# A two-layer trunk: the down projection's Strassen products in groups of three row pairs, an up product after each

## The chip, the cores and the metric

The kernel runs on one core of a Trainium2 chip. The metric is the device time of one execution in microseconds (us). A profile of one further execution gives every instruction of the engines: PE (TensorE, matmuls) with PEld (its weight loads), DVE (VectorE), ACT (ScalarE), POOL (GpSimd) and SP (SyncE, which issues the DMAs).

## The reference, cut to what matters

512 tokens of width 1024 pass through two layers, each a mixer (pooling, then stick-breaking attention) and a squared-ReLU MLP with 4096 hidden rows, all in float32. The MLP is what the change is about:

```python
def sq_relu_mlp(h, w_up, w_down):
    u = jnp.matmul(h, w_up)
    return jnp.matmul(jnp.square(jax.nn.relu(u)), w_down)
...
        h = rms_norm(x, mlp_pre_g[layer])
        x = x + rms_norm(sq_relu_mlp(h, w_up[layer], w_down[layer]), mlp_post_g[layer])
```

## The kernel before

**Precision.** A float32 matrix product is made of three matmuls in the fp32r format: each operand is split into a high part (ACT copies it with rounding, L188, or L118 for a weight) and a low part (DVE subtracts the high part, L189, or L120), and high x high, high x low and low x high are added in PSUM. `mm3` (L209 to L211) and `up_block` (L534 to L536) write these three. One product of 128x128 by 128x512 is called a matmul of 128x512 below.

**Weights.** `want` lists the weights in the order of use. `make` takes the next: SP loads it into one of two raw tiles (L108), ACT and DVE (POOL for four of them) split it. `fill` does so while fewer than four are made ahead; `get` hands one out. The weights of the attention layer get their gains on POOL first (L130).

**The MLP.** The hidden rows stand in 32 blocks of 128. An up product makes one block for all 512 tokens: 24 matmuls, then relu (L489) and square (L490) on ACT. The down product of blocks 0 to 27 is done with Strassen's scheme in Winograd's form, blocks 28 to 31 plainly in `contract`. In the scheme two blocks (2q and 2q+1) make a pair: the two blocks by the two halves of the tokens are the four left quadrants, the two blocks by the two halves of the 1024 output columns the four right ones. Seven products stand for eight. Their left operands (r11, s3, s2, r22, s1, r12, s4) are quadrants or sums of quadrants of the squares, made on POOL (L403 to L406, names s and r in the profile); their right operands (w11, t3, t2, t4, t1, w21, w22) are quadrants or differences of the down weights, made on DVE (L423, names t, xn, spare). All are split into high and low parts.

**Groups.** Before, a group is two pairs (four blocks). `Seven.__init__` loads its four weight blocks, 512 KB each (L384), into the three norm tiles `xn` and a spare tile; `feed` makes the left operands of a pair as its squares come; `prepare` makes the right operands one at a time in eight buffers `w`, called by `make` at most two at a time. `add_to` writes the seven products in one piece: 12 matmuls each (2 token tiles, 2 pairs, 3 matmuls; L456) and two evacuations of a PSUM bank into y (L473 on DVE; for the first sum of a part L471 on ACT). Products that share a PSUM bank keep adding up in it.

**Order.** The program's order is a priority. The library plans the order of each engine's instructions with a simulation of estimated times, so instructions of one group and the next may come interleaved.

**Around it.** `Update` does the sandwich norm: it writes into a norm tile from `xn_tile`, and `transpose` turns it for the next stage (L281). In the attention layer `mix_pair` splits the output of a pair of heads into `ohl` tiles; three of the eight lie in the norm tiles. The out projection then adds them up with `contract`.

Of the kernel before, what the change touches and what calls it, by code (L numbers as in the profile page):

```python
# [10 lines left out]
F32 = mybir.dt.float32  # L11
F32R = mybir.dt.float32r
# [10 lines left out]
GRP = 4  # L23
HEADS = 16
# [37 lines left out]
def trunk(ctx, tc, x, consts, gcol, grow, pw, wup, wdn, wq, wk, wv, wo, out):  # L62
# [26 lines left out]

    def xn_tile():  # L90
        return work.tile([P, D], F32, tag="xn", bufs=3, name=name("xn"))
# [65 lines left out]
    def fill(n=1):  # L157
        if gate[0]:
            behind.update(latest)
        for _ in range(n):  # L160
            if queue and len(made) < ahead and (queue[0][0][0] != "dn" or dn_pool[0] is not None):
                make()
# [130 lines left out]
    def contract(lhs, w, y, first, update=None, tiles=range(T), soon=False):  # L293
# [4 lines left out]
        for t in tiles:  # L298
# [26 lines left out]
            else:  # L325
                product(0, range(last + 1))
            evacuate(0)
# [5 lines left out]
            elif normed and t == T - 1:  # L333
                if not soon:
                    ups[0].transpose()
# [26 lines left out]
    class Seven:  # L362
# [11 lines left out]

        PRODUCTS = (
# [4 lines left out]
        def __init__(self, l, g, mp):  # L380
            self.mp, self.rows, self.left, self.right = mp, [], {}, {}
            self.raw = [xn_tile(), xn_tile(), xn_tile(), spare_tile()]
            for j, raw in enumerate(self.raw):
                nc.sync.dma_start(raw, wdn[l, g * GRP + j])  # L384
            self.rest = self.prepare()

        def feed(self, r):

            q, second = divmod(len(self.rows), 2)
            self.rows.append(r)  # L390
            tile = lambda n, tag: self.mp.tile([P, 2, n], F32R, tag=tag, bufs=2, name=name(tag))
            lo, hi = slice(0, S // 2), slice(S // 2, S)
            if not second:
                a = self.left["r11", q] = tile(S // 2, "r11")
                split(r[:, lo], a[:, 0], a[:, 1])
                return
            a = tile(S, "r2")
            split(r, a[:, 0], a[:, 1])
            self.left["r12", q], self.left["r22", q] = a[:, :, lo], a[:, :, hi]
            r1 = self.rows[-2]  # L400
            sums = self.mp.tile([P, 2, S], F32, tag="s", name=name("s"))
            s2, s3, s1, s4 = sums[:, 0, lo], sums[:, 0, hi], sums[:, 1, lo], sums[:, 1, hi]
            nc.gpsimd.tensor_tensor(out=s3, in0=r1[:, lo], in1=r1[:, hi], op=ALU.subtract)  # L403
            nc.gpsimd.tensor_tensor(out=s1, in0=r1[:, hi], in1=r[:, hi], op=ALU.add)  # L404
            nc.gpsimd.tensor_tensor(out=s2, in0=s1, in1=r1[:, lo], op=ALU.subtract)  # L405
            nc.gpsimd.tensor_tensor(out=s4, in0=r[:, lo], in1=s2, op=ALU.subtract)  # L406
            for n, (x, y) in enumerate((("s2", "s3"), ("s1", "s4"))):
                a = tile(S, f"s{n}")
                split(sums[:, n], a[:, 0], a[:, 1])
                self.left[x, q], self.left[y, q] = a[:, :, lo], a[:, :, hi]  # L410

        def prepare(self):


            def part(key, q, src):
                w = self.right[key, q] = self.mp.tile([P, D], F32R, tag="w", bufs=8, name=name("w"))
                split(src, w[:, NS[0]], w[:, NS[1]])

            def temp():
                return self.mp.tile([P, 512], F32, tag="t", bufs=3, name=name("t"))  # L420

            def combine(out, x, y, op):
                nc.vector.tensor_tensor(out=out, in0=x, in1=y, op=op)  # L423
                return out
# [466 lines left out]
```

## Time and profile before

| | |
|---|---|
| median of 3 runs | 994.76 us (992.62 to 996.26) |
| the profiled execution | 996.64 us, span 994.8 us from the first to the last instruction |
| mean granted TensorE clock | 0.984 |
| moved by DMA | 94.50 MB |

The span has five stretches: the pooling mixer to about 44 us, the first MLP to about 375, attention to about 650, the second MLP to about 970, and the last norm and store. A line of the profile names the source line, the engine, the operation, output and inputs by the program's names, shapes, and count; then busy time, the mean of one in ns, and the idle time just before with what ended it.

### The profile page before, as it was taken

The page shows a single profiled execution, that of the slowest core. Times are in us where ns is not written, and L with a number is a line of the kernel's source. Part 1 is how long each engine was busy: PE and PEld are TensorE (multiplying, and loading weights), DVE is VectorE, ACT ScalarE, POOL GpSimd, SP SyncE. Part 2 cuts the span into 40 slices and gives each one's busy share as a digit, 9 for nine tenths or more (in the row PEclk, how much of TensorE's full clock was granted, in tenths as well). Part 3 has the DMA queues.
Part 4 walks back from the last instruction along what each step waited for, and adds up shares of the span by engine and source line. Part 5 has one row for each costly group of instructions (what it writes and reads, how often), then busy time and mean ns, then how long its engine had stood idle before and what let it go on. Part 6 is the DMA issues. An engine that isn't in the chain of part 4 may idle for free.

```text
span 994.8 us, 12988 instructions
## 1 busy us (share of the span) xinstructions
PE 954.4 (96%) x4823; PEld 810.8 (82%) x4823; DVE 780.6 (78%) x1067; ACT 557.0 (56%) x1005; POOL 252.2 (25%) x238
## 2 busy tenths in 40 slices
PE   7898999999999999999999999989999999999997
PEld 5896888888888888888788988788888888888886
DVE  5987788878877747488688889989778878888636
ACT  5656546456455446566667576658556455464532
POOL 1642202112021147241252300436212021121103
PEclk8998999999999999999999999999999999999999
DMA  7254323323232230112222221144323233231202
GB/s 267 85 162 135 106 86 107 109 103 106 85 111 81 85 127 22 62 45 64 64 73 69 64 72 65 65 148 149 110 102 111 84 125 105 85 127 64 64 22 85
DMA packets 26991, 94.50 MB, mean 95 GB/s; under 512 B 3120, under 2 KB 3504, under 8 KB 26928
## 3 DMA queue, kind: packets, MB, share of 16 engines
q1 hardware_dynamic: 26928, 93.68, 28.2%
q8 instruction: 38, 0.62, 0.2%
q14 instruction: 25, 0.20, 0.1%
HBM read 91.57 MB, written 2.10 MB: 94 GB/s over the span
## 4 chain that ended last, share of the span: by engine, by line
PE 76%; DVE 8%; ACT 4%; POOL 3%; issue 2%; DMA 1%; POOLq 0%; DVEq 0%; ACTq 0%
PE ps L456 26%; PE ps L535 13%; PE ps L536 13%; PE ps L534 13%; PE ps L209 3%; PE ps L210 2%; PE ps L211 2%; DVE e L752 2%; PE ps L780 1%; DVE l L120 1%; PE ps L770 1%; POOL y L234 1%; DMA xn<-in_wdn 1%; ACT h L118 1%; DVE x L240 1%
## 5 line engine op out<-in xcount | busy, mean ns | idle before, releaser
L535 PE MATMUL ps<-xnl,h 128*128 128x512 f32 (+1 forms) x712 | 262.0, 369 | 4.1 <-DVE xnl L189 4.1
L536 PE MATMUL ps<-xnh,l 128*128 128x512 f32 (+1 forms) x712 | 262.1, 369 | 0.5 <-DVE l L120 0.5
L534 PE MATMUL ps<-xnh,h 128*128 128x512 f32 (+1 forms) x712 | 261.0, 369 | 0.0
L120 DVE TENSOR_TENSOR l<-raw,h 128x1024 fp32r<-128x1024 f32 x101 | 128.8, 1276 | 48.5 <-ACT h L118 48.3
L456 PE MATMUL ps<-w,s 128*128 128x512 f32 x672 | 163.4, 394 | 2.1 <-ACT s L188 1.5
L535 PEld LDWEIGHTS ps<-xnl,h 128*128 128x128 f32 x712 | 134.8, 189 | 26.1 <-DVE xnl L189 4.3
L536 PEld LDWEIGHTS ps<-xnh,l 128*128 128x128 f32 x712 | 134.8, 189 | 22.8 <-DVE l L120 0.7
L456 PEld LDWEIGHTS ps<-w,s 128*128 128x128 f32 x672 | 127.2, 190 | 31.1 <-ACT s L188 2.7
L534 PEld LDWEIGHTS ps<-xnh,h 128*128 128x128 f32 x712 | 134.2, 190 | 21.9
L473 DVE TENSOR_TENSOR y<-ps,y 128x512 f32<-128x512 f32 x180 | 120.1, 688 | 40.5 <-PE ps L456 39.3
L118 ACT CAST h<-raw 128x1024 fp32r<-128x1024 f32 x105 | 110.4, 1053 | 63.9 <-PE ps L535 32.4
L456 PE MATMUL ps<-w,r 128*128 128x512 f32 x504 | 124.3, 390 | 2.4 <-DVE r L189 2.4
L188 ACT CAST w<-t 128x512 fp32r<-128x512 f32 x112 | 69.2, 622 | 80.8 <-PE ps L456 61.0
L456 PEld LDWEIGHTS ps<-w,r 128*128 128x128 f32 x504 | 94.7, 188 | 22.4 <-DVE r L189 2.8
L404 POOL TENSOR_TENSOR s<-r,r 128x256 f32<-128x256 f32 x28 | 28.2, 1008 | 323.9 <-ACT r L490 323.9
L130 POOL TENSOR_TENSOR raw<-raw,gc 128x512 f32<-128x512 f32 x48 | 69.9, 1477 | 145.7 <-DMA raw<-in_wv 68.9
L188 ACT CAST w<-xn 128x512 fp32r<-128x512 f32 x56 | 34.9, 624 | 90.1 <-PE ps L456 80.0
L189 DVE TENSOR_TENSOR w<-t,w 128x512 fp32r<-128x512 f32 x112 | 76.5, 705 | 0.7 <-ACT w L188 0.7
L188 ACT CAST s<-s 128x512 fp32r<-128x512 f32 x56 | 34.6, 620 | 45.6 <-POOL s L405 37.6
L189 DVE TENSOR_TENSOR s<-s,s 128x512 fp32r<-128x512 f32 x56 | 42.5, 763 | 22.0 <-ACT s L188 17.5
L189 DVE TENSOR_TENSOR r<-r,r 128x512 fp32r<-128x512 f32 (+1 forms) x60 | 47.2, 789 | 11.7 <-ACT r L188 11.6
L752 DVE TENSOR_TENSOR_SCAN e<-u,begin 128x1280 f32<-128x1280 f32 x16 | 47.5, 2968 | 8.7 <-ACT u L746 8.5
(138 smaller groups left out, 1577.9 us busy)
## 6 DMA issues: line engine op xcount, KB each, us to landing
raw<-in_wup SPq DMA_DIRECT2D x64, 512.0 KB, 3.5
xn<-in_wdn SPq DMA_DIRECT2D x42, 512.0 KB, 3.6
spare<-in_wdn SPq DMA_DIRECT2D x14, 512.0 KB, 4.1
raw<-in_wdn SPq DMA_DIRECT2D x8, 512.0 KB, 3.5
raw<-in_wv SPq DMA_DIRECT2D x8, 512.0 KB, 3.4
raw<-in_wk SPq DMA_DIRECT2D x8, 512.0 KB, 3.5
raw<-in_wq SPq DMA_DIRECT2D x8, 512.0 KB, 3.5
raw<-in_wo SPq DMA_DIRECT2D x8, 512.0 KB, 3.5
```

Source lines behind the costliest of these rows:

```text
L118: nc.scalar.copy(hi, raw)
L120: on.tensor_tensor(out=lo, in0=raw, in1=hi.bitcast(F32), op=ALU.subtract)
L130: nc.gpsimd.tensor_tensor(out=v[:, h], in0=v[:, h], in1=g[:, h].broadcast_to((P, n // 2, D // n)), op=ALU.mult)
L188: latest["act"] = nc.scalar.copy(hi, src)
L189: latest["dve"] = nc.vector.tensor_tensor(out=lo, in0=src, in1=hi.bitcast(F32), op=ALU.subtract)
L209: nc.tensor.matmul(dst, ah, bh, start=start, stop=False)
L456: nc.tensor.matmul(bank, r[:, a], w_[:, NS[b]], start=start and q == 0 and k == 0, stop=q == 1 and k == 2, skip_group_check=True,)
L473: nc.vector.tensor_tensor(out=part, in0=bank, in1=part, op=ALU.add)
L534: nc.tensor.matmul(pu[:, cols], wh[:, k, :], xnh[:, k, cols], start=k == 0, stop=False)
L535: nc.tensor.matmul(pu[:, cols], wh[:, k, :], xnl[:, k, cols], start=False, stop=False)
L536: nc.tensor.matmul(pu[:, cols], wl[:, k, :], xnh[:, k, cols], start=False, stop=k == KC - 1)
L752: nc.vector.tensor_tensor_scan(out=e[:, ::-1], data0=u[:, 1:][:, ::-1], data1=begin[:, ::-1], initial=0.0, op0=ALU.mult, op1=ALU.max,)
```

## The change

The 14 pairs are taken in five groups of 2, 3, 3, 3 and 3 pairs. `load` brings the first blocks of all pairs of a group with one DMA into a tile w1, the second blocks with another into the three norm tiles, which are now one tile xn3. `left` and `right` make the operands of one product for all pairs at once: the sums overwrite the squares and the weights or one tile e, and go into one of two buffers `a` (left) and `w` (right). `mlp` writes one product, one up product of the next group, and then the operands of the product after the next one; the operands of the next group's first two products come at the end of a group. `product` has 18 matmuls with three pairs, 12 with two. The four plain down weights go into pieces of w1, e and w. The squares of a group lie in one tile r. The transpose of the first tile at the end of the first MLP is written ahead of an evacuation, and the `ohl` tiles get five buffers of their own and a part of e.

```diff
+GROUPS = (2, 3, 3, 3, 3)
+MOST = max(GROUPS)
...
+    xn3 = work.tile([P, 3, D], F32, tag="xn3", name="xn3")
+    turn = [0]
+
     def xn_tile():
-        return work.tile([P, D], F32, tag="xn", bufs=3, name=name("xn"))
+        turn[0] += 1
+        return xn3[:, turn[0] % 3]
...
-            return [dn_pool[0].tile([P, D], F32R, tag="w", bufs=8, name=name(x)) for x in "hl"]
+            return dn_pool[0].pop(0)
...
+            if normed and t == T - 1 and not soon:
+                ups[0].transpose()
             evacuate(0)
...
-                if not soon:
-                    ups[0].transpose()
                 product(1, [0])
...
+        def load(self, second):
+            n = self.n
+            if second:
+                w = self.w2 = xn3
+            else:
+                w = self.w1 = self.mp.tile([P, MOST, D], F32, tag="w1", name=name("w1"))
+            src = wdn[self.l, self.first : self.first + 2 * n].rearrange("(n k) p d -> k p n d", k=2)
+            nc.sync.dma_start(w[:, :n], src[1 if second else 0])
+        def squares(self):
+            self.r = self.mp.tile([P, 2, MOST, S], F32, tag="r", bufs=2, name=name("r"))
+        def part(self, b):
+            return self.r[:, b % 2, b // 2]
+        def left(self, i):
+            n, key = self.n, self.PRODUCTS[i][1]
             lo, hi = slice(0, S // 2), slice(S // 2, S)
+            r11, r21, r12, r22 = (self.r[:, k, :n, h] for k in range(2) for h in (lo, hi))
+            if i == 0:
+                self.s1 = self.mp.tile([P, MOST, S // 2], F32, tag="s1", name=name("s1"))
+            s1 = self.s1[:, :n]
+            sub = lambda out, x, y, op=ALU.subtract: nc.gpsimd.tensor_tensor(out=out, in0=x, in1=y, op=op)
+            if key == "s3":
+                sub(s1, r21, r22, ALU.add)
+                sub(r21, r11, r21)
+                sub(r11, s1, r11)
+            elif key == "r22":
+                sub(r11, r12, r11)
+            src = {"r11": r11, "s3": r21, "s2": r11, "r22": r22, "s1": s1, "r12": r12, "s4": r11}[key]
+            a = self.mp.tile([P, 2, MOST, S // 2], F32R, tag="a", bufs=2, name=name("a"))
+            split(src, a[:, 0, :n], a[:, 1, :n])
+            return a
+        def right(self, i):
+            n, key = self.n, self.PRODUCTS[i][2]
+            w11, w12, w21, w22 = (w[:, :n, h] for w in (self.w1, self.w2) for h in NS)
+            if i == 0:
+                self.e = self.mp.tile([P, MOST, 512], F32, tag="e", name=name("e"))
+            e = self.e[:, :n]
+            combine = lambda out, x, y, op=ALU.subtract: nc.vector.tensor_tensor(out=out, in0=x, in1=y, op=op)
+            if key == "t3":
+                combine(e, w22, w12)
+            elif key == "t2":
+                combine(e, e, w11, ALU.add)
+            elif key == "t4":
+                combine(e, w21, e)
+            elif key == "t1":
+                combine(w12, w12, w11)
+            src = {"w11": w11, "t3": e, "t2": e, "t4": e, "t1": w12, "w21": w21, "w22": w22}[key]
+            w = self.mp.tile([P, 2, MOST, 512], F32R, tag="w", bufs=2, name=name("w"))
+            split(src, w[:, 0, :n], w[:, 1, :n])
+            return w
+        def make(self, i):
+            self.operands[i] = self.left(i), self.right(i)
+        def product(self, i, y, first):
+            a, w = self.operands.pop(i)
+            at, _, _, tokens, half = self.PRODUCTS[i]
+            start = at not in self.banks
+            if start:
+                self.banks[at] = [ps(), ps()]
+            for t, bank in enumerate(self.banks[at]):
+                for q in range(self.n):
+                    for k, (x, z) in enumerate(((0, 0), (0, 1), (1, 0))):
                         nc.tensor.matmul(
+                            bank, a[:, x, q, TS[t]], w[:, z, q], start=start and q == 0 and k == 0,
+                            stop=q == self.n - 1 and k == 2, skip_group_check=True,
                         )
+                part = y[2 * tokens + t][:, NS[half]]
+                if first and (tokens, half, t) not in first:
+                    nc.scalar.copy(part, bank)
+                    first.add((tokens, half, t))
+                else:
+                    nc.vector.tensor_tensor(out=part, in0=bank, in1=part, op=ALU.add)
...
+        groups = [Seven(l, firsts[g], n, mp) for g, n in enumerate(GROUPS)]
...
+        groups[0].load(0)
+        groups[0].squares()
         need(0, 1)
-        first = [(ps(), get(("up", l, j))) for j in range(GRP)]
+        n0 = 2 * GROUPS[0]
+        first = [(ps(), get(("up", l, j))) for j in range(n0)]
         for j, (pu, w) in enumerate(first):
-            if j == GRP - 1:
+            if j == n0 - 1:
                 need(2, 3)
+                groups[0].load(1)
             up_block(pu, w, slice(0, S // 2))
         for j, (pu, w) in enumerate(first):
             up_block(pu, w, slice(S // 2, S))
             up(j, pu)
-            feed(j)
-        for g in range(last):
-            up((g + 1) * GRP)
-            del squares[:GRP]
-            group.make(1)
-            group.add_to(y, g == 0)
-            group = Seven(l, g + 1, mp) if g + 1 < last else None
-            feed(0)
-            for j in range(1, GRP):
-                up((g + 1) * GRP + j)
-                feed(j)
-        w = [get(("dn", l, last * GRP + j)) for j in range(GRP)]
+        for i in range(2):
+            groups[0].make(i)
+        for g, group in enumerate(groups):
+            coming = groups[g + 1] if g + 1 < len(groups) else None
+            if coming:
+                coming.squares()
+            ups = list(range(firsts[g + 1], firsts[g + 1] + 2 * GROUPS[g + 1]) if coming else range(plain, NJ))
+            for i in range(7):
+                group.product(i, y, written if g == 0 else None)
+                if i + 2 < 7:
+                    if ups:
+                        up(ups.pop(0))
+                    group.make(i + 2)
+                    if i + 2 == 4 and coming:
+                        coming.load(0)
+                    if i + 2 == 6 and coming:
+                        coming.load(1)
+                else:
+                    if ups:
+                        up(ups.pop(0))
+                    if coming:
+                        coming.make(i + 2 - 7)
+                    elif i == 5:
+                        piece = lambda tag, k, bufs=1: mp.tile([P, k, D], F32R, tag=tag, bufs=bufs, name=name("dn"))
+                        w, e, x, z = piece("w1", 3), piece("e", 1), piece("w", 3, 2), piece("w", 3, 2)
+                        dn_pool[0] = [
+                            [w[:, 0], w[:, 1]], [w[:, 2], e[:, 0]], [x[:, 0], x[:, 1]], [x[:, 2], z[:, 0]],
+                        ]
+        w = [get(("dn", l, j)) for j in range(plain, NJ)]
+        dn_pool[0] = None
         fill(ahead)
-        contract(squares, w, y, False, update)
-        dn_pool[0] = None
+        contract(squares[1:], w, y, False, update)
...
-            if p in (2, 3, 4):
-                both = work.tile([P, D], F32R, tag="xn", bufs=3, name=name("ohl"))
+            if p < PAIRS - 1:
+                both = ap.tile([P, D], F32R, tag="ohl", bufs=5, name=name("ohl"))
             else:
-                both = ap.tile([P, D], F32R, tag="ohl", bufs=3, name=name("ohl"))
+                both = ap.tile([P, NSEG], F32R, tag="e", name=name("ohl"))[:, :D]
...
-    nc = bacc.Bacc("TRN2", target_bir_lowering=False, num_devices=1, dynamic_dma_scratch_size=1024)
+    nc = bacc.Bacc("TRN2", target_bir_lowering=False, num_devices=1, dynamic_dma_scratch_size=256)
```

More of the change, by code (lines that the diff above doesn't have):

```diff
@@ L160, in fill @@
         for _ in range(n):
[L161 removed]
+            if queue and len(made) < ahead and (queue[0][0][0] != "dn" or dn_pool[0]):
                 make()
@@ L480, in mlp @@
         y = y_tiles()
-        last = NJ // GRP - 1
-        squares, group = [], Seven(l, 0, mp)
+        firsts = [2 * sum(GROUPS[:g]) for g in range(len(GROUPS))]
+        plain = 2 * sum(GROUPS)
+        groups = [Seven(l, firsts[g], n, mp) for g, n in enumerate(GROUPS)]
+        squares = []
+        written = {None}
         def up(j, pu=None):
```

108 lines of the change are left out of this document (16 added, 92 removed).

## The prediction

> **What bounds the kernel now.** I read the page first, then the busy time by stretch, then the chain of waits and TensorE's timeline where the stretches were not full.
>
> ```profile
> span 994.8 us, 12988 instructions
> PE 954.4 (96%) x4823; PEld 810.8 (82%) x4823; DVE 780.6 (78%) x1067; ACT 557.0 (56%) x1005; POOL 252.2 (25%) x238
> ```
>
> The matmul engine is busy 96% of the span, so all that can be won without removing matmuls is in the 40.4 us in which it is not busy, and in time at a lower clock. The stretches say where that lies:
>
> ```profile
> 44.00:126.00 82.00, 78.08 (x430) 66.97 (x429) 66.69 (x94) 51.39 (x92) 26.14 (x22) 0.96 0.40 132
> 126.00:340.00 214.00, 214.00 (x946) 177.20 (x945) 174.02 (x254) 110.98 (x176) 35.74 (x40) 1.00 0.29 96
> 640.00:700.00 60.00, 53.70 (x330) 47.74 (x329) 52.69 (x78) 41.88 (x82) 27.85 (x19) 0.97 0.42 135
> 700.00:940.00 240.00, 240.00 (x1060) 198.76 (x1059) 193.63 (x280) 127.36 (x202) 45.93 (x47) 1.00 0.29 98
> 123.67:164.47 40.80, 40.80 (x181) 33.78 (x180) 33.43 (x49) 21.41 (x35) 6.96 (x8) 1.00 0.31 104
> ```
>
> The columns are the stretch, its length, busy time of PE, PEld, DVE, ACT and POOL with instruction counts, granted clock, DMA share and GB/s. In both MLPs, once they run, PE is full at clock 1.00. The last row is exactly one group of two pairs: 84 product matmuls and four up products of 24, 180 in 40.80 us, so 0.2267 us for each 128x512 matmul. DVE, at 33.4 of 40.8 us, is the next engine and waits for nothing that PE feels.
>
> Losses stand only where an MLP begins. This is PE in the first group of the first MLP:
>
> ```profile
> 75.95 1.52 PE L456 MATMUL ps<-w,r 128*128 128x512 f32 x6
> 77.31 0.61 PE L456 MATMUL ps<-w,s 128*128 128x512 f32 x2
> 78.47 1.20 PE L456 MATMUL ps<-w,s 128*128 128x512 f32 x4 [0.54 <-DVE s L189]
> 79.50 1.07 PE L456 MATMUL ps<-w,r 128*128 128x512 f32 x4
> 83.00 1.22 PE L456 MATMUL ps<-w,r 128*128 128x512 f32 x2 [2.42 <-DVE r L189]
> 84.26 6.93 PE L456 MATMUL ps<-w,s 128*128 128x512 f32 x18
> 91.03 0.61 PE L456 MATMUL ps<-w,r 128*128 128x512 f32 x2
> ...
> 80.00:83.00 3.00, 0.58 (x4) 0.15 (x2) 3.00 (x4) 0.84 (x1) 2.84 (x3) 0.93 0.27 108
> 83.00:85.00 2.00, 1.96 (x4) 1.14 (x5) 2.00 (x2) 2.00 (x5) 0.53 (x1) 0.50 0.87 262
> 85.00:95.00 10.00, 10.00 (x36) 7.55 (x35) 6.68 (x11) 6.89 (x14) 1.04 (x1) 0.78 0.31 111
> ...
> 123.83 8.61 PE ps L456 x38
> ```
>
> Counted, these are 38 product matmuls, and an up product follows at 91.48. They take 15.53 us; the same 38 in the next group (the last line, of the chain) take 8.61. So 6.92 us are lost: 2.96 in two waits for operands that DVE was late with, and 3.96 because the clock was at 0.50 after the 2.42 us wait and 0.78 on average to 95 us. The waits come because, in that first group, DVE and ACT make all seven products' operands as soon as data arrive, with nothing made ahead.
>
> [...]
>
> In the second MLP the same block is:
>
> ```profile
> 683.52 2.88 PE L456 MATMUL ps<-w,r 128*128 128x512 f32 x12
> 686.24 1.52 PE L456 MATMUL ps<-w,s 128*128 128x512 f32 x6
> 689.30 4.52 PE L456 MATMUL ps<-w,s 128*128 128x512 f32 x18 [1.53 <-ACT s L188]
> 693.65 0.61 PE L456 MATMUL ps<-w,r 128*128 128x512 f32 x2
> 694.10 0.39 PE L534 MATMUL ps<-xnh,h 128*128 128x512 f32 x1
> ```
>
> 10.58 us, of which 1.97 are lost.
>
> **The change, part by part.** *Matmuls.* Before: 7 groups of 7 products x 12 = 588 a layer. After: 42 a pair x 14 pairs = 588. The same 32 up products and four plain blocks remain. So the floor in the full stretches doesn't move, and the number of groups is worth nothing to PE.
>
> *Evacuations.* 14 a group, 7 groups before and 5 after, 28 fewer a layer. Durations for this and what follows:
>
> ```profile
> L473 DVE TENSOR_TENSOR y<-ps,y 128x512 f32<-128x512 f32 x180 | 120.1, 688 | 40.5 <-PE ps L456 39.3
> L120 DVE TENSOR_TENSOR l<-raw,h 128x1024 fp32r<-128x1024 f32 x101 | 128.8, 1276 | 48.5 <-ACT h L118 48.3
> L118 ACT CAST h<-raw 128x1024 fp32r<-128x1024 f32 x105 | 110.4, 1053 | 63.9 <-PE ps L535 32.4
> L189 DVE TENSOR_TENSOR w<-t,w 128x512 fp32r<-128x512 f32 x112 | 76.5, 705 | 0.7 <-ACT w L188 0.7
> L188 ACT CAST w<-t 128x512 fp32r<-128x512 f32 x112 | 69.2, 622 | 80.8 <-PE ps L456 61.0
> L489 ACT ACTIVATE r<-ps 128x512 f32<-128x512 f32 x64 | 37.6, 590 | 12.7 <-PE ps L536 12.6
> L490 ACT ACTIVATE r<-r 128x512 f32<-128x512 f32 x64 | 40.4, 632 | 1.6
> L405 POOL TENSOR_TENSOR s<-s,r 128x256 f32<-128x256 f32 x28 | 30.1, 1073 | 2.2
> L234 POOL TENSOR_TENSOR y<-y,grow 128x512 f32<-128x512 f32 x12 | 19.7, 1648 | 116.5 <-ACT xn L192 116.5
> L120 POOL TENSOR_TENSOR l<-raw,h 128x1024 fp32r<-128x1024 f32 x4 | 10.1, 2526 | 14.1 <-ACT h L118 14.1
> ```
>
> 56 evacuations x 0.688 = 38.5 us leave DVE, all beside PE work, worth nothing directly.
>
> *Operands for three pairs in one instruction.* The columns made are the same (1,792 left and 3,584 right a pair); only the instruction grows. By the lines through the rows above, my estimates are: DVE 0.99 us for 768 columns and 1.85 for 1,536; ACT 0.84 and 1.48; POOL 2.1 for 768, between 1.65 and 2.53. A step (one product of 18 matmuls, 4.08 us, and one up product of 24, 5.44 us) is 9.52 us of PE. In it DVE has two evacuations 1.38, left low part 0.99, right low part 1.85, in four of seven a combination 1.85, and the up weight's low part 1.28: at most 7.35. ACT has 0.84 + 1.48 + 0.59 + 0.63 + 1.05 = 4.6. Both fit.
>
> *Two operand buffers where right operands had eight.* Operands i+2 can only be written once product i has left its buffers, and are due when product i+2 starts: 5.44 + 4.08 + 5.44 = 14.96 us later. The chain is about 0.84 + 1.48 + 1.85 = 4.2 us, under 9 with the rest of DVE's step in front of it. Cost nothing; that cover is gone only where no up product lies between, which is the last group's products 4 to 6 (it has four up products for seven steps). There product 6 has 4.08 us against 4.2 us and a second evacuation: 0 to 1 us late, I take 0.5, twice, so +1.0 us.
>
> *The border between groups.* The second product needs s3, two sums on POOL over squares of the group's last up product. That up product ends 4.08 + 4.08 + 5.44 = 13.6 us before the second product starts. Chain: 0.59 + 0.63 + 2.1 + 2.1 + 0.84 + 0.99 = 7.3 us. Behind the waiting s3 cast on ACT stand the right cast of the same product and the next up product's relu; PE doesn't need these for another 5 us or more. Nothing.
>
> *Weights.* One load of 1.5 MB where there were 512 KB loads:
>
> ```profile
> raw<-in_wup SPq DMA_DIRECT2D x64, 512.0 KB, 3.5
> ```
>
> Three times 3.5 is 10.5 us at most. The first tile of a group is free after product 4's operands are made and is used again three steps (28 us) later; the second after product 6's, used again 19 us later; 4 us of making go off both. Both fit, in the short first group (12-matmul products) with about 2 us to spare. On SP the load waits for DVE, and the up weights behind it wait along; they have a step each. The four plain down weights now wait for the pieces at product 5: two fit in tiles long free, the third has 1.05 + 1.28 us against product 6's 4.08, the fourth's low part 1.28 against 18 matmuls, 4.08. Nothing; if the loads were not issued early, 3.5 + 2.3 = 5.8 us a layer.
>
> *The start of an MLP.* This is the term that counts. Before the first product only two products' operands are made, no longer seven, and an up product stands after each product. The s3 chain with two pairs: 0.59 + 0.63 + 2 x 1.65 + 0.62 + 0.71 = 5.9 us after the fourth up product, against 2.72 (12 matmuls) + 5.44 = 8.16 us. So in the first MLP both waits and the slow clock after them should go: -6.9 us (bounds 0, if other waits take their place, and -6.9). In the second MLP the loss is 1.97 us, but POOL's first sum there was long:
>
> ```profile
> 672.91 6.22 POOL L403 TENSOR_TENSOR s<-r 128x256 f32<-128x256 f32 x1 [12.57 <-ACT r L490]
> 679.08 1.72 POOL L404 TENSOR_TENSOR s<-r,r 128x256 f32<-128x256 f32 x1
> ```
>
> If that recurs in front of the s3 chain, 5.9 + (6.2 - 1.1) = 11.0 us against 8.16 leave a wait of 2.8. Bounds -2.0 and +2.8; I take -1.0, since the sums were also made once in the first MLP without such a start.
>
> *The attention layer.* The projected heads get five tiles of their own; the three norm tiles are free for the last projection. There PE has this wait:
>
> ```profile
> PE ps L535 <- DVE xnl L189: 4.1, 1, 4.1
> ```
>
> It is an order of DVE's queue, which a new plan can shuffle either way: -4.1 to +4.1, taken as 0. Moving the transpose ahead of an evacuation at the end of the first MLP only reorders ACT and DVE, within the same bounds.
>
> *Sum.* -6.9 - 1.0 + 1.0 = -6.9 us. The profiled execution took 996.64 us (span 994.8 and 1.84 around it), which gives 989.7; it lay 1.9 us above the median of 994.76, so the median forecast is 987.9, say 988. The forecast's own range goes from all gains (-6.9 - 2.0 - 4.1: 982) to 993.
>
> **The rivals.** *The start stays as it was, or loses elsewhere.* The order in which instructions are issued is not that of the program: a plan by estimated times decides, and the profile shows it, for a group's 84 product matmuls are written in one piece and came as 38, 34 and 12 with up products between. So the first group can meet another wait, the 6.22 us sum in the second MLP among them. Between 0 and -5 us: 990 to 996, say 993.
>
> *Slower: the left operands are late at each border between groups.* Three pairs' sums are now one POOL instruction on the path from squares to second product. The row at 679.08 has 1.72 us for 256 columns; at three times that, a sum takes 5.2 us and the chain is 13.5 of the 13.6 us. From there on every microsecond of queue on ACT or DVE is a PE wait, at eight borders. At 2 us each it is +16, less 6.9: 1004 us. A wait of 2.4 us would bring the half clock of the first group's row, 4 us more each. Against it: the mean of that sum is 1.07, and DVE has more idle time than before. [...]
>
> *The products don't come one by one.* If the plan draws up products ahead, products stand back to back with 4.08 us of cover instead of 14.96 and each of them waits; three a group at 1 us, ten groups: +30, 1018 us. For it: the blocks seen before. Against: up weights are made only four ahead.
>
> **How the numbers follow.** Forecast 0.52, start not won 0.25, borders late 0.18, blocks 0.05. About 0.5% (5 us) is what a measurement of this kernel can tell from no change. So faster 0.52, same 0.25, slower 0.23. The range takes the forecast's low end, 981, and the border case to 1004, with the blocks and the tails left out.
>
> **What would show it.** Right: L456's first 38 matmuls without a listed wait, clock 1.00 from 70 to 126 us, about 70 evacuations a layer, PE still full at 0.2267 us a matmul between. Wrong: PE waits at the second product of each group, named after POOL's sums or the left casts, a clock below 1.00 in the middle of an MLP, or a wait of over 3 us at the second MLP's start. If PE is full in the middle and the gain is missing, the start was not its place.

## The result, and the profile after

The change made the kernel slower: 1005.72 us median of 4 runs (1003.57 to 1007.02) against 994.76 (992.62 to 996.26), a ratio of 1.011 with a 95% interval of 1.0084 to 1.0136. 988.0 had been forecast, with 981 to 1004 as the range. The profiled execution took 1007.02 us with a span of 1005.1, 10.3 us longer than before's.

First the page's head and the same stretches as before, with one new stretch, 340 to 405 us, from the end of the first MLP into the attention layer.

```profile
span 1005.1 us, 12276 instructions
PE 954.9 (95%) x4823; PEld 812.2 (81%) x4823; DVE 740.9 (74%) x771; ACT 529.0 (53%) x837; POOL 232.1 (23%) x166
```

The stretches of after (columns as in the prediction):

```profile
44.00:126.00 82.00, 77.72 (x433) 68.16 (x432) 53.49 (x59) 43.57 (x67) 15.21 (x10) 0.96 0.45 148
126.00:340.00 214.00, 214.00 (x946) 177.20 (x945) 161.14 (x135) 102.62 (x116) 40.41 (x16) 1.00 0.27 91
340.00:405.00 65.00, 53.84 (x258) 45.39 (x257) 42.99 (x55) 32.57 (x61) 30.10 (x40) 0.89 0.23 73
640.00:700.00 60.00, 54.46 (x336) 48.64 (x335) 45.65 (x66) 37.00 (x70) 24.47 (x20) 0.97 0.32 106
700.00:940.00 240.00, 240.00 (x1060) 198.72 (x1060) 175.66 (x150) 117.05 (x136) 41.92 (x16) 1.00 0.31 106
```

The new stretch in the kernel before:

```profile
340.00:405.00 65.00, 62.24 (x329) 53.66 (x328) 39.46 (x57) 33.56 (x68) 30.54 (x41) 0.97 0.23 73
```

In the middle of both MLPs PE is full, with the same 946 and 1060 matmuls as before: there the change costs and brings nothing. The first MLP's start is as full as it was (77.72 us against 78.08, clock 0.96 both times). The new loss is in 340 to 405: 8.40 us less of PE work, and a clock of 0.89. The list of PE's waits names it (engine and line waiting, engine, output and line waited for; us in all, times, longest):

```profile
PE ps L289 <- ACT xn L280: 12.2, 2, 11.2
PE ps L462 <- ACT a L196: 4.5, 2, 3.4
```

One wait of 11.2 us, in front of the first transpose after the first MLP. It was 0.92 us before.

**A table of lost time.** To place all of it, I set against the start of chosen matmuls the time that the matmuls issued until then need at full clock (0.2267 us for 512 columns, 0.12 for 256, as they follow each other in the full stretches), and took differences. "Start" runs from the first up product to the 38th product matmul, "transition" from the last product matmul to the first transpose behind it, "attention" from there to the second MLP's first up product, "tail" from the last matmul to the end of the span. All in us, one profiled execution each; the kernels e1 to e12 (there is no e5) are those of the experiments. From one execution to another the start varies: e8 and e9, whose code there is the same, differ by 3.5 us in it, and e1 differs from before by 2.1.

```
                        start  middle  transition  attention  2nd start  tail    span
before                    8.7     0.0         1.1       31.5        8.5   7.3   994.8
after                     8.2     0.0        11.3       30.8        7.2   9.7  1005.1
e1 before, late opening   6.6     0.0         1.9       31.0        9.1   7.3   994.1
e2 no gains               8.4     0.0         8.6       23.0        7.3   9.7   995.3
e3 attention first        8.5     0.3         9.6       32.6        6.6   9.7  1005.2
e4 transpose back         8.0     0.0        13.9       32.8        8.6   9.7  1010.3
e6 early down, two        8.5     0.0        11.4       30.8        7.3   9.7  1006.2
e7 early down, all        8.1     0.0         6.5       31.8        7.3   7.1   999.2
e8 e7 + up weight         3.0     0.0         6.6       30.8        7.3   7.1   994.6
e9 e8 + attention first   6.5     0.0         0.0       31.7        6.6   7.2   989.2
e10 e9 + gain row later   2.6     0.4         0.0       31.5        8.2   7.2   987.7
e11 e9 + relu first       1.6     0.0         0.0       31.8        6.8   7.2   986.6
e12 both                  2.8     0.0         0.0       30.5        6.7   7.1   984.7
```

Transition +10.2, tail +2.4, second start -1.3, attention -0.7, start -0.5 and the first up product 0.25 later: 10.3 us, the whole difference of the spans.

**The transition, read in the timeline.** The timeline of before, at the end of the first MLP: the first sum of the plain blocks is added to y (DVE), tile 0's x is updated, normed (ACT) and transposed (PE).

```profile
371.62 1.89 DVE L316 TENSOR_TENSOR y<-ps,y 128x512 f32<-128x512 f32 x3 [2.02 <-PE ps L211]
377.35 1.41 DVE L240 SCALAR_TENSOR_TENSOR x<-y,stat,x 128x512 f32<-128x512 f32 x2
382.38 2.56 ACT L272 ACTIVATE xn<-x,stat 128x512 f32<-128x512 f32 x4 [0.21 <-POOL stat L205]
383.15 1.27 PE L281 MATMUL ps<-ident,xn 128*128 128x128 f32 x8 [0.92 <-ACT xn L272]
```

The same in after, with the low parts of the third and fourth plain down weights (dn), product 6's last matmuls (L462) and what POOL does (timeline):

```profile
359.96 1.22 DVE L128 TENSOR_TENSOR dn<-raw,dn 128x1024 fp32r<-128x1024 f32 x1 [0.17 <-ACT dn L126]
363.43 3.79 PE L462 MATMUL ps<-w,a 128*128 128x512 f32 x16
367.87 1.22 DVE L128 TENSOR_TENSOR dn<-raw,dn 128x1024 fp32r<-128x1024 f32 x1
372.79 4.04 POOL L138 TENSOR_TENSOR raw<-raw,gc 128x512 f32<-128x512 f32 x4 [5.74 <-DMA raw<-in_wv]
374.06 1.89 DVE L324 TENSOR_TENSOR y<-ps,y 128x512 f32<-128x512 f32 x3 [3.84 <-PE ps L219]
376.79 3.99 POOL L242 TENSOR_TENSOR y<-y,grow 128x512 f32<-128x512 f32 x2
383.16 2.18 DVE L248 SCALAR_TENSOR_TENSOR x<-y,stat,x 128x512 f32<-128x512 f32 x2
392.35 1.33 ACT L280 ACTIVATE xn<-x,stat 128x512 f32<-128x512 f32 x2 [1.07 <-POOL stat L213]
393.12 1.97 PE L289 MATMUL ps<-ident,xn 128*128 128x128 f32 x8 [11.16 <-ACT xn L280]
```

PE's plain work ends at 393.12 - 11.16 = 381.96 us, as before (382.23). But the first sum is added at 374.06, so 7.9 us of matmuls are left to cover the norm, where 10.6 were. The fourth plain down weight (the third row) is ready only at 369.09, since its low part lies in the buffer of product 6, whose last matmuls end at 367.22. And the norm itself is longer: four instructions with gains of the attention weights (L138) stand ahead of y's gain (L242) on POOL, and the first x update comes 5.8 us later than before. From the first sum to the transpose it is 19.1 us where it was 11.5. So of the 10.2 us by which the wait grew, 2.7 are less cover and 7.5 a longer norm. In the second MLP the same weight is late, at 978.74, and the first sum with it (timeline of after; in before the first sum was added 14.1 us ahead of the last matmul, at 973.33 and 987.44, here 10.5 us ahead of it, at 995.42):

```profile
978.74 1.22 DVE L128 TENSOR_TENSOR dn<-raw,dn 128x1024 fp32r<-128x1024 f32 x1
984.93 2.48 DVE L324 TENSOR_TENSOR y<-ps,y 128x512 f32<-128x512 f32 x4 [4.97 <-PE ps L219]
```

**The start, read in the timeline.** The 38 matmuls no longer lose 6.9 us, but the first of them waits, and the clock falls. ACT, POOL, DVE and PE in after's timeline:

```profile
62.23 1.05 ACT L196 CAST w<-w 128x1024 fp32r<-128x1024 f32 x1 [5.05 <-DMA w<-in_wdn]
67.93 1.05 ACT L196 CAST w<-e 128x1024 fp32r<-128x1024 f32 x1 [3.20 <-DVE e L436]
73.59 0.61 ACT L196 CAST a<-r 128x512 fp32r<-128x512 f32 x1
64.31 2.50 POOL L128 TENSOR_TENSOR l<-raw,h 128x1024 fp32r<-128x1024 f32 x1 [9.66 <-ACT h L126]
64.51 3.38 DVE L436 TENSOR_TENSOR e<-xn,w 128x1024 f32<-128x1024 f32 x1
74.25 2.08 PE L462 MATMUL ps<-w,a 128*128 128x512 f32 x4 [3.36 <-ACT a L196]
```

And the stretch behind that wait:

```profile
74.00:80.00 6.00, 5.75 (x14) 4.49 (x15) 4.27 (x4) 2.99 (x5) 4.41 (x3) 0.50 0.49 165
```

ACT ran its queue in order here: a relu was done at 64.73 us, and its square ran only at 68.88, behind the cast at 67.93. The queue held a cast that waited 5.05 us for the first down weights, then one that waited 3.20 us for a combination on DVE, and the relus of the up products, from which the first product's left operand is made, stood behind them.

### The profile page after: what moved, and what is told of

Same layout as the page of the kernel before. It is cut to its first block, busy times and chain, and to the rows that moved or that the text cites. A ratio compares the mean times of both kernels' runs of the same rounds, so it can differ in the third digit from the quotient of the medians.

```text
span 1005.1 us, 12276 instructions
## 1 busy us (share of the span) xinstructions
PE 954.9 (95%) x4823; PEld 812.2 (81%) x4823; DVE 740.9 (74%) x771; ACT 529.0 (53%) x837; POOL 232.1 (23%) x166
## 4 chain that ended last, share of the span: by engine, by line
PE 81%; DVE 8%; ACT 4%; POOL 3%; DMA 2%; issue 2%; SPq 0%; POOLq 0%; DVEq 0%; ACTq 0%
PE ps L462 27%; PE ps L556 13%; PE ps L557 13%; PE ps L555 13%; PE ps L217 3%; PE ps L218 3%; PE ps L219 3%; PE ps L801 1%; DVE l L128 1%; DVE e L773 1%; POOL y L242 1%; ACT h L126 1%; PE ps L791 1%; PE ps L289 1%; PE ps L759 1%
## 5 line engine op out<-in xcount | busy, mean ns | idle before, releaser
L462 PE MATMUL ps<-w,a 128*128 128x512 f32 x1176 | 279.1, 390 | 4.5 <-ACT a L196 4.5
L462 PEld LDWEIGHTS ps<-w,a 128*128 128x128 f32 x1176 | 221.1, 188 | 50.7 <-ACT a L196 4.9
L471 DVE TENSOR_TENSOR y<-ps,y 128x512 f32<-128x512 f32 x124 | 84.7, 687 | 60.5 <-PE ps L462 60.3
L138 POOL TENSOR_TENSOR raw<-raw,gc 128x512 f32<-128x512 f32 x48 | 66.2, 1401 | 165.6 <-DMA raw<-in_wv 91.5
L196 ACT CAST a<-r 128x768 fp32r<-128x768 f32 (+1 forms) x60 | 47.7, 796 | 101.3 <-PE ps L462 64.0
L197 DVE TENSOR_TENSOR a<-r,a 128x768 fp32r<-128x768 f32 (+1 forms) x60 | 63.4, 1057 | 12.1 <-ACT a L196 12.1
L197 DVE TENSOR_TENSOR w<-e,w 128x1536 fp32r<-128x1536 f32 (+1 forms) x30 | 64.2, 2140 | 10.6 <-ACT w L196 10.1
L196 ACT CAST w<-e 128x1536 fp32r<-128x1536 f32 (+1 forms) x30 | 42.0, 1399 | 40.2 <-DVE e L436 27.6
L417 POOL TENSOR_TENSOR r<-r 128x768 f32<-128x768 f32 (+1 forms) x20 | 42.6, 2128 | 39.7 <-DVE a L197 38.9
L242 POOL TENSOR_TENSOR y<-y,grow 128x512 f32<-128x512 f32 x12 | 21.1, 1761 | 114.0 <-ACT xn L200 114.0
L197 DVE TENSOR_TENSOR w<-w,w 128x1536 fp32r<-128x1536 f32 (+1 forms) x20 | 33.0, 1649 | 8.8 <-ACT w L196 8.8
L217 PE MATMUL ps<-h,xnh 128*128 128x256 f32 x128 | 36.6, 286 | 1.7 <-DVE kl L715 1.4
```

The source lines that it names most:

```text
L138: nc.gpsimd.tensor_tensor(out=v[:, h], in0=v[:, h], in1=g[:, h].broadcast_to((P, n // 2, D // n)), op=ALU.mult)
L196: latest["act"] = nc.scalar.copy(hi, src)
L197: latest["dve"] = nc.vector.tensor_tensor(out=lo, in0=src, in1=hi.bitcast(F32), op=ALU.subtract)
L217: nc.tensor.matmul(dst, ah, bh, start=start, stop=False)
L417: sub = lambda out, x, y, op=ALU.subtract: nc.gpsimd.tensor_tensor(out=out, in0=x, in1=y, op=op)
L462: nc.tensor.matmul(bank, a[:, x, q, TS[t]], w[:, z, q], start=start and q == 0 and k == 0, stop=q == self.n - 1 and k == 2, skip_group_che ...
```

## The experiments

Kernels measured together share the runs of the kernel before, whose median was 995.81 us beside e1 to e4, 996.47 beside e6 to e9, 995.13 beside e10 to e12. Ratios are to it, with 95% intervals.

### e1: the kernel before, with its plain down weights opened late

```diff
-        dn_pool[0], gate[0] = mp, False
+        dn_pool[0], gate[0] = None, False
...
-        w = [get(("dn", l, last * GRP + j)) for j in range(GRP)]
+        dn_pool[0] = mp; w = [get(("dn", l, last * GRP + j)) for j in range(GRP)]
```

> The kernel before, with one part of the change: the four plain down weights may only be made after the last group's products. Theory A (late down weights hold back the attention weights and their gains on POOL, and bunch the sums of the plain blocks): the wait ahead of the first transpose after the first MLP grows from 0.9 us to some 8 to 11, the time after the last matmul from 7.3 to 9 or more, in all +8 to +12 us. Theory B (what costs is the new order of products and up products in the last group, or the moved transpose): no change, within 2 us of before.

Measured: 996.42 us (995.04 to 999.54), ratio 1.001 (0.9995 to 1.0026); transition 1.9 us. The place in the program at which these weights are opened costs nothing, as long as their buffers are free: the plan still makes them early.

### e2: the kernel after, without the gains of the attention weights

```diff
-        return scaled
+        return None
```

> The changed kernel without the gains that POOL multiplies into the attention weights; that part of the computation is left out. Theory A: the wait ahead of the first transpose after the first MLP falls from 11.2 us to 3 or less, since the sums of squares and norms on POOL then have nothing ahead of them; 8 to 11 us less in all, a little more from the attention layer. Theory B (the moved transpose, or the sums of the plain blocks coming too late): the wait stays at 7 us or more, and the total falls by less than 4.

Measured: 997.14 us (994.50 to 999.21), ratio 1.001 (0.9995 to 1.0026), 8.6 us less than after. But little of it is in the transition (timeline of e2):

```profile
376.68 2.47 DVE L324 TENSOR_TENSOR y<-ps,y 128x512 f32<-128x512 f32 x4
391.10 1.97 PE L289 MATMUL ps<-ident,xn 128*128 128x128 f32 x8 [8.47 <-ACT xn L280]
```

The wait falls from 11.16 to 8.47 us; the rest of the gain (attention 30.8 to 23.0 in the table) is in the attention layer, where before has the gains too. So with no gain at all on POOL the larger part of the wait stays: the gains are not the only cause. Nor does the run take the attention weights themselves away: their low parts still stood on DVE ahead of the first sum, which came 2.6 us later than in after.

### e3: the kernel after, attention weights made ahead of the plain down weights

```diff
+    n = next(k for k, q in enumerate(queue) if q[0][0] == "dn")
+    queue[n : n + 8] = queue[n + 4 : n + 8] + queue[n : n + 4]
```

> The changed kernel with the first four attention weights (two of v, one of k, one of q) ahead of the four plain down weights in the order of loading. Theory A: their gains run on POOL before the first MLP's last norm, the wait ahead of the transpose falls from 11.2 us to under 4, total -6 to -10 us. Theory B: no change, or slower by 1 to 3 us as the down weights come later still.

Measured: 1006.26 us (1005.37 to 1006.99), ratio 1.0104 (1.0087 to 1.0121): no gain, although no gain of a weight stood on POOL between 349 and 385 us. The down weights now came later still (timeline of e3):

```profile
369.16 1.22 DVE L128 TENSOR_TENSOR dn<-raw,dn 128x1024 fp32r<-128x1024 f32 x1
375.35 3.08 DVE L327 TENSOR_TENSOR y<-ps,y 128x512 f32<-128x512 f32 x5 [4.97 <-PE ps L222]
```

The first sum is added at 375.35, 1.3 us later than in after. The wait in front of the transpose falls only from 11.16 to 9.45 us, and the attention layer takes back as much (30.8 to 32.6 in the table).

### e4: the kernel after, the transpose back behind the evacuation

```diff
-            if normed and t == T - 1 and not soon:
-                ups[0].transpose()
             evacuate(0)
...
+                if not soon:
+                    ups[0].transpose()
                 product(1, [0])
```

> The changed kernel with the transpose at the first MLP's end written where it was before, behind the evacuation. Theory A: within 1 us of the changed kernel, as the planned order differs in a few lines only. Theory B (the transpose moved ahead blocks TensorE's queue): the 11.2 us wait shrinks by 2.7 us or more, the 12 matmuls that stand behind it.

Here the last tile's squares overwrite the first tile's normed values before they are transposed, since both lie in one slot of xn3. Measured: 1010.94 us (1009.52 to 1012.76), ratio 1.0152 (1.0129 to 1.0175), 5 us slower than after; PE's list has "PE ps L289 <- ACT xn L200: 13.7", a wait for those squares. Since the wait is now for these squares, this run doesn't test the moved line by itself. e9 below does: it keeps the line, and no wait is left there.

### e6 and e7: earlier places for the plain down weights

e6 gives the first two of the four their pieces (w1 and e) once product 4's operands are made. e7 gives all but the last low part a place that is free once product 6's operands are made, with three pieces of the squares' tile r; the last low part takes the buffer of product 5 in place of product 6. The edit of e7:

```diff
+                    if i + 2 == 6 and not coming:
+                        piece = lambda tag, k, bufs=1: mp.tile([P, k, D], F32R, tag=tag, bufs=bufs, name=name("dn"))
+                        w, e, r = piece("w1", 3), piece("e", 1), piece("r", 3, 2)
+                        dn_pool[0] = [[w[:, 0], w[:, 1]], [w[:, 2], e[:, 0]], [r[:, 0], r[:, 1]]]
+                        fill(3)
...
                     elif i == 5:
+                        x = piece("w", 3, 2)
+                        dn_pool[0] += [[r[:, 2], x[:, 0]]]
+                        fill()
```

> The kernel after; only the first two of the four plain down weights get their place earlier (pieces w1 and e opened once product 4's operands are made, instead of after product 5); the third and fourth still wait for the operands of products 5 and 6. Theory P (the plain blocks' sums end late because the last two down weights wait for the buffers of the last two products, so that the first evacuation leaves about 8 us of matmuls to cover a norm chain of about 19 us, where the kernel before had 10.6 us for a chain of about 11 us): no gain, 1004 to 1007 us, the wait in front of the transpose 9 us or more. Rival Q (all four weights wait in one line for cast and subtraction, and the first two hold up the others): 2 to 4 us faster, 1001 to 1004.

> The kernel after; all four plain down weights but the last one's low part get pieces that are free once product 6's operands are made (w1, e and the squares' buffer r); the last low part takes the buffer of product 5. Theory P: the first evacuation comes 2 to 4 us earlier against the end of the matmuls, the wait in front of the transpose falls from 11.2 to 3 to 6 us, the tail by 1 to 2 us: 996 to 1000 us. Rival G (gains on GpSimd between the sums are the cause): the wait stays at 9 us or more, 1004 to 1007.

Measured: e6 1008.32 us (1007.66 to 1008.82), ratio 1.0124 (1.0108 to 1.0139): nothing. e7 999.56 us (997.60 to 1001.08), ratio 1.0026 (1.0006 to 1.0045), 8.8 us faster than e6 beside it. The fourth weight's low part moved from 368.76 us in e6 (367.87 in after) to 361.27, the third's from 360.85 (359.96) only to 359.53, and the first two were early in all of them: what counts is the one buffer of product 6. In the table that is 4.9 us of the transition and 2.6 of the tail. The timeline of e7:

```profile
361.27 1.22 DVE L128 TENSOR_TENSOR dn<-raw,dn 128x1024 fp32r<-128x1024 f32 x1
366.86 3.02 POOL L138 TENSOR_TENSOR raw<-raw,gc 128x512 f32<-128x512 f32 x2 [0.40 <-DMA raw<-in_wv]
370.99 1.23 DVE L128 TENSOR_TENSOR l<-raw,h 128x1024 fp32r<-128x1024 f32 x1 [1.41 <-ACT h L126]
372.14 1.88 DVE L324 TENSOR_TENSOR y<-ps,y 128x512 f32<-128x512 f32 x3
388.68 1.97 PE L289 MATMUL ps<-ident,xn 128*128 128x128 f32 x8 [6.30 <-ACT xn L280]
976.38 1.37 DVE L324 TENSOR_TENSOR y<-ps,y 128x512 f32<-128x512 f32 x2 [0.90 <-PE ps L219]
```

The tail is back at 7.1 us. In the transition a wait of 6.30 us is left (expected were 3 to 6), and the rows say why: the first sums now wait on DVE behind an attention weight's low part, which waits for ACT's cast, which waits for that weight's gains on POOL.

### e8: e7, and the fifth up weight's low part on DVE

```diff
-ON_POOL = {("up", 0, j) for j in (0, 1, 2, 4)}
+ON_POOL = {("up", 0, j) for j in (0, 1, 2)}
```

> The one before this, and the low part of the first layer's fifth up weight is made by VectorE instead of GpSimd. Theory S (the stall of 3.36 us at the first Strassen product comes from the 3.38 us that VectorE takes for the first combination beside GpSimd's 2.50 us subtraction): that combination takes about 1.2 us and the stall falls by about 2 us, 1 to 3 us faster than the one before it. Rival (the load of the first down weights, 7.9 us to landing, sets it): within 0.5 us of it.

The timeline of e8:

```profile
64.70 1.23 DVE L436 TENSOR_TENSOR e<-xn,w 128x1024 f32<-128x1024 f32 x1 [0.17 <-DMA xn<-in_wdn]
73.66 1.20 PE L462 MATMUL ps<-w,a 128*128 128x512 f32 x4 [2.01 <-ACT a L196]
```

The combination took 1.23 us where it had taken 3.38 beside POOL's subtraction, and the stall shown is 2.01. But that profile is the fastest of ten runs: the median, 998.93 us (996.35 to 1002.71), ratio 1.0036 (1.0019 to 1.0053), is that of e7, and e9 has the same edit with a stall of 3.00. A gain in time from this edit is not shown.

### e9: e8 with e3's order, and the down weights not held back by it

```diff
-            if queue and len(made) < ahead and (queue[0][0][0] != "dn" or dn_pool[0]):
+            dn = queue and queue[0][0][0] == "dn"
+            if queue and (dn_pool[0] if dn else sum(k[0] != "dn" for k in made) < ahead):
```

> The one before this, and the first four attention weights are made before layer 0's down weights, so that their gains leave GpSimd before the plain blocks' sums. From the run without any gains (2.7 us of the wait): 2 to 3 us faster than the one before it, the wait in front of the transpose under 3 us, 991 to 996 us in all. If the down weights then come late again: no faster than it, or slower by up to 3 us.

Measured: 991.48 us (987.47 to 993.48), ratio 0.9948 (0.9929 to 0.9966), 7.4 us faster than e8 where 2 to 3 were expected. The timeline of e9 at the transition:

```profile
367.12 1.37 DVE L328 TENSOR_TENSOR y<-ps,y 128x512 f32<-128x512 f32 x2 [0.90 <-PE ps L223]
376.36 1.34 ACT L284 ACTIVATE xn<-x,stat 128x512 f32<-128x512 f32 x2 [0.51 <-POOL stat L217]
379.40 1.04 PE L293 MATMUL ps<-ident,xn 128*128 128x128 f32 x8
381.05 4.94 POOL L138 TENSOR_TENSOR raw<-raw,gc 128x512 f32<-128x512 f32 x4
```

The first sum at 367.12 leaves 12.3 us of matmuls; the norm is done at 377.7; the transpose follows without a wait, and the next gains start behind it all. e3's edit alone left 9.45 us of the wait and gained no time, e7's left 6.3 us, both together take all 11.2: either cause alone keeps more than half of the wait.

### e10, e11 and e12: the start

e10 issues the second layer's gain row after the second group's first load, so that it no longer stands ahead of the first group's load in SP's queue. e11 issues the casts of the next up weights on ACT after the first group's squares. e12 is both.

```diff
+        with tc.issue_after(loads[2].ins):
+            gpre1 = gain_row(R_MLP_PRE1, spare_tile())
```

```diff
+            if j >= 2 * GROUPS[0]:
+                fill()
...
+        behind["act"] = latest.pop("square")
+        fill(ahead)
+        behind.pop("act")
```

> The kernel e9_after_r_up4_att_first; only the later layer's gain row is loaded after the second group's first down weights, so that the first group's load no longer stands behind it in SyncE's queue, where it waits for the spare tile until 53.2 us. Theory L (the load of the first down weights, issued at 53.6 and landed at 61.8 us, holds ScalarE's queue and so the first products): the load is issued up to 3 us earlier, ScalarE's wait of 5.3 us shrinks by as much, and the stall of 3.0 us at the first Strassen product goes: 1 to 4 us faster than e9. Theory R (a cast of a following up weight stands ahead of the third relu on ScalarE and waits until the last up product has freed its buffer, at 70.25 us): the stall stays at 2 to 3 us, within 0.7 us of e9.

> The kernel e9_after_r_up4_att_first; at the start of each MLP the casts of the next up weights are issued on ScalarE only after the squares of the first group. Theory R: the third relu follows its product by about 1 us, the first Strassen product starts when the up products end, the stall of 3.0 us falls below 0.7 and the clock of 0.83 in 70 to 80 us returns to 1: 2 to 5 us faster than e9 (986 to 990 us). Theory L: the stall stays above 2 us. If the up weights then come late for the products that follow: a wait in an up product at 76 to 80 us, no gain.

> Both of the two before this. If R holds alone: as e11_relu_first within 0.7 us. If both matter: 1 to 3 us faster than it.

Measured: e10 988.92 us (986.56 to 989.76), ratio 0.9930 (0.9918 to 0.9943); e11 987.93 (986.43 to 989.32), 0.9922 (0.9909 to 0.9934); e12 987.01 (986.48 to 988.72), 0.9922 (0.9908 to 0.9935). The timeline of e10:

```profile
50.62 0.39 SPq L407 DMA_DIRECT2D w<-in_wdn  x1
58.89 1.05 ACT L200 CAST w<-w 128x1024 fp32r<-128x1024 f32 x1 [1.80 <-DMA w<-in_wdn]
71.30 1.20 PE L468 MATMUL ps<-w,a 128*128 128x512 f32 x4 [0.50 <-ACT a L200]
```

The load goes out 3.0 us earlier than in e9 (53.59), and the stall falls from 3.00 to 0.50. In e11 the load is as late as in e9 (54.02), and the first product doesn't wait either; the only wait left is one of 0.44 us for an up weight (timeline of e11):

```profile
74.98 0.50 PE L568 MATMUL ps<-xnh,l 128*128 128x512 f32 x1 [0.44 <-DVE l L128]
```

So each theory named a real delay, and removing either one takes the stall: it is ACT's queue, filled by casts that wait for something, with the relus behind. This is read from the stalls: in time the gain over e9 (ratio 0.9948) is small, and the intervals overlap. The two don't add up. e12 is 8.1 us faster than the kernel before and, by the two ratios, about 19 us faster than the change as it was made.

## Why the prediction was wrong

**The step that failed: "Nothing" for the plain down weights.** The prediction set the fourth weight's low part, 1.28 us, against 18 matmuls of 4.08 us, as many as product 6 has. But that part is written into product 6's own buffer, so it can only follow the last matmul of product 6, and nothing of the MLP but the plain blocks is left to cover it. PE had other plain blocks to go on with, so no wait shows at this point, and a comparison of the weight with PE alone finds none. What it delays is the first finished sum, and behind that stands the whole norm, 19.1 us of which 11.2 had no matmuls beside them. The price of 5.8 us a layer was given for another case, loads that are issued late, and was kept out of the sum and of the rivals; e7 against e6 gives 4.9 us at the end of the first MLP and 2.6 at the end of the second. Shown by e7 against e6 (8.8 us in the medians), and by e1: late in the program isn't late, a buffer that isn't free is.

**Second, "the attention layer, taken as 0".** The layer itself was 0.7 us better, within the bounds. But its weights are made behind the plain down weights in one queue, so later down weights push its gains on POOL, and the casts behind them, into the norm at the end of the first MLP. In after SyncE loaded the second of them only at 369.11 us, when the fourth low part had been made from its raw tile; in e7 at 362.51. The prediction counted only a shuffle of queues there, within 4.1 us either way; the transition grew by 10.2. Shown by e2 (2.7 us of the wait) and e9 against e8 (6.6 us of the transition, 7.4 in the medians).

**The start, -6.9 us.** The 38 matmuls lost 2.9 us where they had lost 6.9, so "made ahead" worked for them; but the up products before lost 5.3 where they had lost 1.8. The rival "the start stays as it was, or loses elsewhere" was right here: -0.5 in all. It said that the first group can meet another wait, but not which: the first group's load stood behind a gain row in SP's queue, and ACT's casts ahead of the relus. With either mended the loss is 1.6 to 2.8 us, so most of the term of -6.9 was there to be had: 6.0 us in e10, 5.5 in e11 (8.7 - 1.6, less 1.6 by which its first up product came later), 6.1 in e12. That e12's median of 987.01 is close to the 988 that was forecast for the change itself confirms nothing, since that kernel has several more edits.

**The second start**, taken as -1.0, was -1.3; the 6.22 us sum did not recur (POOL's first sum there took 1.80). **The last group's product 6**, +1.0, cost nothing: "middle" is 0.0 to the last product matmul. **Operand costs and the middle** came as worked out:

```profile
L471 DVE TENSOR_TENSOR y<-ps,y 128x512 f32<-128x512 f32 x124 | 84.7, 687 | 60.5 <-PE ps L462 60.3
L197 DVE TENSOR_TENSOR w<-w,w 128x1536 fp32r<-128x1536 f32 x16 | 28.1, 1755 | 3.4 <-ACT w L196 3.4
L196 ACT CAST a<-r 128x768 fp32r<-128x768 f32 x48 | 40.3, 839 | 94.2 <-PE ps L462 62.5 <-POOL r L417 30.9 <-DVE y L471 0.8
L417 POOL TENSOR_TENSOR r<-r 128x768 f32<-128x768 f32 x16 | 37.4, 2337 | 31.2 <-DVE a L197 30.6
```

These are rows of after's groups, for 512, 1,536 and twice 768 columns. The estimates had been 0.688 (a row of before), 1.85, 0.84 and 2.1 us. The slower rival, late operands at the borders, gave 1004 us for a reason that wasn't there: no PE wait stands at a border. The time was near it by luck, from the sum of other things. The "mean of that sum", 1.07 us, that the prediction set against the 1.72 us row was that of another line, L405; L404, the row's own, has a mean of 1.01.

## What to carry to other kernels

When a buffer is reused for the last operand of a stage, don't ask whether the engine that consumes it has other work, but when the first result of the next dependent chain is finished, and how much work is left then to cover that chain. Read each engine's queue from its head. In after a cast on ScalarE waited 5.05 us for a load and a later one 3.20 us for a combination, and a square whose relu was done at 64.73 us ran only at 68.88, behind them; in e10 the first group's load, no longer behind a gain row's on SyncE, went out at 50.62 us, in e9 at 53.59. Two causes in series hide each other in single experiments: in the kernel's time, mending one alone showed 0 (e3) or 9 us (e7 against e6); mending both took the whole wait (e9).

## What the runs showed of the hardware that was not expected

**The clock behind a wait.** In the first MLP's start, take the waits of five kernels in front of a product: behind 0.50 us (e10) and 2.01 us (e8) the clock stayed at 1.00; with 2.42 us (before), 3.00 us (e9) and 3.36 us (after) it was at 0.50: to about 89 us in before, from 74 to 80 in after, and for 3.4 us in e9. But the length of the wait alone doesn't decide it. In before a wait of 1.67 us, in front of a matmul of the attention layer at 523.65 us, shorter than e8's, was followed by half clock as well. These are stretches of before around that wait, and then the stretches of e8 around its wait, which ended at 73.66 us:

```profile
519.50:522.91 3.41, 1.83 (x15) 1.36 (x13) 2.78 (x5) 2.22 (x5) 0.00 (x0) 1.00 0.42 133
522.91:526.33 3.42, 1.74 (x7) 1.26 (x8) 3.39 (x6) 2.72 (x7) 2.04 (x2) 1.00 0.42 139
526.33:529.74 3.41, 3.41 (x15) 3.31 (x14) 1.73 (x4) 3.12 (x8) 2.02 (x2) 0.50 0.09 37
72.00:74.00 2.00, 0.34 (x2) 0.30 (x2) 1.36 (x2) 1.88 (x4) 0.00 (x0) 1.00 0.61 225
74.00:76.00 2.00, 2.00 (x10) 1.65 (x9) 1.06 (x2) 1.69 (x3) 0.15 (x1) 1.00 0.81 244
```

In the traces of before and after the stretches at half clock lasted 3.41, 6.83 or, in after from 383.97 us, 13.65 us (the last of each aside, which the end cuts off). In before they begin, from 38.22 us on, at 82.60, 400.04, 526.33 and 652.62: 13, 93, 37 and 37 times 3.41 us apart. What decides which of the waits are followed by half clock was not shown.

**VectorE beside GpSimd.** One combination of 128x1024 took 3.38 us in after, from 64.51 to 67.89, with a GpSimd subtraction of 2.50 us beside it, from 64.31 to 66.81; it took 1.23 us in e8, where GpSimd ran nothing at that time. After's next two combinations of this size, with GpSimd idle, took 1.23 us (at 67.93) and 1.22 (at 70.32). What makes it longer was not shown.
